# Matmul with batch norm on one core: two blocks of the third tile stored by GpSimd's converting transfers, one more raw block of the fifth tile, and a held half-block stored in two partition ranges

## The chip, the cores and the metric

The kernel runs on one core of one Trainium2 chip. The metric is the device time of one execution in microseconds (us). Three runs of the kernel before gave 205.51, 205.90 and 206.09 us, median 205.90. One further execution was profiled; its own numbers stand in the section on the profile below.

## The reference

The reference multiplies x (16 x 512 rows of 1024, float32) by a weight of 1024 x 768 and normalises each of the 768 output columns over all 8192 rows:

```python
y = np.matmul(x, weight)
mean = np.mean(y, axis=(0, 1), keepdims=True)
var = np.var(y, axis=(0, 1), keepdims=True)
y_norm = (y - mean) / np.sqrt(var + eps)
return (gamma * y_norm + beta).astype(np.float32)
```

No output of a column can be written before the whole column has been multiplied, since mean and variance need all its rows. The output is 25.17 MB of float32.

## The kernel before

The 768 columns are six tiles of 128, numbered 0 to 5; the 8192 rows are 16 chunks of 512. What the texts call the third tile is number 2, the fifth is number 4. GpSimd loads x with converting transfers (float32 in HBM, bf16 in SBUF, L404), VectorE transposes it (L429, L436), and TensorE multiplies. Tiles 0 and 1 are made together with rows on the partitions (L511); tiles 2 to 5 are made transposed, with the 128 columns on the partitions and 512 rows along the free dimension (L576). The multiplying goes on tile after tile, and while tile n is multiplied, tile n-1 is normalised and stored. Two chunks make a block of 1024 rows by 128 columns, 512 KB in float32; a tile has eight blocks, numbered by their first chunk 0, 2, 4 ... 14.

The work of one multiplied chunk: VectorE takes the statistics of the PSUM bank (L712), then ScalarE copies the bank to SBUF as bf16 (L716). There are eight PSUM banks. When the last chunk of a tile is in, its scale and shift are made (L977 to L1007), and then each block of it goes out in one of these ways, since the transposed result has to be turned back:

- **"xact"** (tiles 2 and 3): normalise in place (ScalarE L1024 for tile 2, VectorE L1027 for tile 3), a transposing DMA from SyncE into a bf16 slot of the SBUF ring (L1221), ScalarE converts that to a float32 slot of the ring (L1233), SyncE stores (L1203).
- **"xpool"** (no block of the kernel before): the same as far as the transposing DMA; then GpSimd stores the bf16 slot with a transfer that converts to float32 on its way (L1227). There is no float32 slot and no work for ScalarE.
- **"pe"** (tile 4): normalise in place (L1027), eight 128 x 128 transposes on TensorE (L1045), ScalarE copies the PSUM bank to a float32 slot (L1211), SyncE stores (L1203).
- **raw** (blocks listed in RAW): the bf16 block is turned by a transposing DMA before it is normalised (L1107); when scale and shift are known, they are spread over the partitions as rows (VectorE L1142 and L1143, seven small copies per tile on GpSimd or ScalarE L1146, ScalarE L1159), VectorE multiplies (L1175), GpSimd adds (L1179), SyncE stores (L1183).

The blocks of tiles 0 and 1 go out through VectorE and GpSimd (L938, L943) and SyncE (L947).

The last block of tile 4 is **held** (function held_block): its two halves of 512 rows are transposed on TensorE after the last matmul, copied by ScalarE (L1253) and stored by SyncE (L1256, 256 KB each) while the statistics of tile 5, the last, are finished (L1311 to L1327). Then tile 5 is normalised (L1351), transposed (L1045), copied (L1364) and stored in eleven pieces (L1367).

Work is put in order by a planner in the kernel (function arrange): each task has engines with a cost, a due time and the slots that it takes, and the planner deals the tasks out to the engines by its own costs. Each engine then runs its list in that order and waits on semaphores; a task that may run on one of two engines (L1146 and L548 among them) is put where the planner finds room. All stores of SyncE are in one list, and a transposing DMA in that list stands in line with the stores. The ring holds six float32 slots of a block; a slot comes free when the store that reads it has landed.

Of the kernel before, what the change touches and what calls it, by code (L numbers as in the profile page):

```python
# [227 lines left out]
def kernel(  # L228
# [9 lines left out]
    nc = tc.nc  # L238
# [9 lines left out]
    P = 128  # L248
# [19 lines left out]
    PAD = 50  # L268
    HELD = 1
    PAIRED = 1  # L270
    ASTAT = {2:tuple(range(4,16))}
    RC = C - 2
    XT, YB, SQ = C - EARLY, 29, 3
    ADDED = (0,6,16,28,40)
    PARTED, LATE, SINGLE = (4,5,7,8,9,10), (12,13,14,15), (2,3,6)
    MODE = {2:'xact',3:'xact',4:('pe',)*8}
    MODE = {nt: m if isinstance(m, tuple) else (m,) * (C // GY) for nt, m in MODE.items()}
    RAW, RAWADD, RAWDUE = {2:(0,2),3:(0,2),4:(0,2,4)}, {2:'POOL',3:'POOL',4:'POOL'}, {2:14.0,3:8.0,4:8.0}
    LAST = (12,13,14,15)
    SOON = ((11, {"POOL": (1.06, 1.1)}),)  # L280
    RING = 3 * CH // 32 * KQ // 2
# [3 lines left out]
    out_flat = out.flatten_outer_dims()  # L285
# [9 lines left out]
    def seq(bi):  # L295

        ins = bi.ins
        prev = last.get(ins.engine)
        if prev is not None:
            tc.add_manual_dep(  # L300
                ins, prev,
                mybir.DependencyInfo(mybir.DependencyClass.NoSync, mybir.DependencyReason.DATA),
                reason="order",
            )
        last[ins.engine] = ins.name
        return bi
# [21 lines left out]
    fin = singles.tile([P, 9 + 6 * len(PIECES)], f32)  # L328
    psums = {nt: singles.tile([P, 2, C], f32, name=f"psums{nt}") for nt in ASTAT}
    sums = {nt: singles.tile([P, 4 + 6 * C], f32, name=f"sums{nt}") for nt in ASTAT}  # L330
    for nt in ASTAT:
        seq(nc.vector.memset(sums[nt][:, 1:2], float(len(ASTAT[nt]) * CH)))
    msq = singles.tile([P, GA], f32)
# [23 lines left out]
    def task(prio, engines, emit, deps=(), lock=False, **kw):  # L357
        t = Task(prio, engines, emit, deps, **kw)
        t.lock = lock
        tasks.append(t)  # L360
        return t

    def dve(occ):
        return {"DVE": (occ, occ + 0.09)}

    def act(occ):
        return {"ACT": (occ, occ + 0.11)}
# [4 lines left out]
    def pe(occ):  # L372
        return {"PE": (occ, occ + 0.03)}
# [4 lines left out]
    def piece(slot):  # L378
        return ring[:, slot.at:slot.at + slot.words]
# [28 lines left out]
    def load_affine(eng):  # L408
        seq(nc.vector.memset(gamma_sb, 0.0))
        seq(nc.vector.memset(beta_sb, 0.0))  # L410
        for nt in range(0, NT, 2):
            n = 2 if nt < 2 * PAIRED else 1
            for i in range(nt, nt + 2, n):
# [35 lines left out]
    for kind, n, *n1 in order:  # L449
# [10 lines left out]
        rows = n1[0] if kind == "p" else QR if kind == "x" else CH  # L460
        m0 = n if kind == "p" else n * rows
        if m0 == M // 2:
            affine_loads = affine = task(t, {"SP": (5.0, 7.0)}, load_affine, [x_ready[m0 // CH - 3, 0, JW]])
        slot = Slot(rings, rows // 32 * KQ // 2)
# [221 lines left out]
    def y_of(nt, c):  # L686
        return y_col.setdefault((nt, c // GY), Slot(ys))
# [11 lines left out]
    def stats_of(nt):  # L699
        return stats[:, (nt - GA) * C:(nt - GA + 1) * C]  # L700
# [3 lines left out]
    def col_stats(nt, c, slot, t):  # L704
        now = clock[0]

        def bn(eng):
            dst = fin[:, 3:9] if (nt, c) == (NT - 1, C - 2) else stats_of(nt)[:, c, :]
            if nt in ASTAT:
                i = 4 + 6 * [j for j in range(C) if j not in ASTAT[nt]].index(c)  # L710
                dst = sums[nt][:, i:i + 6]
# [195 lines left out]
    def spread_rows(i):  # L907
        def emit(eng):
            a_ps = psum.tile([P, CH], f32, tag="b")
            aff[i] = a_ps[:, 0:NA]  # L910
            for a in range(GA):
                spread(a_ps[:, a * P:(a + 1) * P], (scale, shift)[i], a)
        return emit
# [11 lines left out]
    p0 = task(U, pe(0.45), spread_rows(0), [sc], takes=[a0_slot])  # L925
    p1 = task(U, pe(0.45), spread_rows(1), [sr], takes=[a1_slot])
# [93 lines left out]
    def norm(nt, c, n=1):  # L1020
        def emit(eng):
            part = y(nt, c, n)
            if eng == "ACT":
                seq(nc.scalar.activation(  # L1024
                    part, part, AF.Identity, bias=shift[:, nt:nt + 1], scale=scale[:, nt:nt + 1]))
            else:
                seq(nc.vector.tensor_scalar(  # L1027
                    part, part, scale[:, nt:nt + 1], shift[:, nt:nt + 1],
                    op0=ALU.mult, op1=ALU.add))
        return emit  # L1030

    def turn_block(prio, nt, m0, count, deps, uses):

        bank = Slot(banks)
        todo = []

        def step():
            if not todo:
                o_ps = psum.tile([P, count, P], bf16, tag="b")
                bank.tile = o_ps  # L1040
                for s in range(count):
                    c, i = divmod(m0 // P + s, RT)
                    todo.append((o_ps[:, s], y(nt, c)[:, i * P:(i + 1) * P]))
            dst, src = todo.pop(0)
            seq(nc.tensor.transpose(dst, src, ident))  # L1045

        def emit(eng):
            for _ in range(emit.task.count):
                step()

        emit.step = step
        t = task(prio, pe(0.0555 * count), emit, deps, takes=[bank], uses=uses)
        emit.task = t
        turns[t] = [count, count]
        return t, bank
# [136 lines left out]
    def col_block(nt, c, due, fin_task, held=False):  # L1192
# [12 lines left out]
        a = task(due, act(1.144) if nt == GA else dve(0.45), norm(nt, c, GY), [fin_task] + keeps, nt > GA, uses=[yslot])  # L1205
        if MODE[nt][c // GY] == "pe":
            b, bank = turn_block(due + 0.5, nt, m0, count, [a], [yslot])
# [11 lines left out]
        def xbar(eng):  # L1219
# [3 lines left out]
        b = task(due + 0.5, {"SP": (1.4, 1.4)}, xbar, [a], dma=XBAR,  # L1223
                 takes=[t_slot] + ([slot] if MODE[nt][c // GY] == "xact" else []), uses=[yslot])
        if MODE[nt][c // GY] == "xpool":
            def store_x(eng):
                seq(nc.gpsimd.dma_start(dst(), t_slot.o))  # L1227
# [13 lines left out]
    def held_block(nt, c, due, fin_task, last_mm, root_task):  # L1241
        yslot = y_of(nt, c)
        keeps = [col_end[nt, c + i][1] for i in range(GY)]
        count = RT
        a = task(due - 20.0, dve(0.45), norm(nt, c, GY), [fin_task] + keeps, True, uses=[yslot])
        for i in range(GY):
            slot = Slot(rings, count * P)
            m0 = (c + i) * CH
            b, bank = turn_block(due - 1.0 + 0.1 * i, nt, m0, count, [a, last_mm], [yslot])

            def copy(eng, slot=slot, bank=bank):
                slot.o = piece(slot).rearrange("p (s n) -> p s n", n=P)
                seq(nc.scalar.copy(slot.o, bank.tile))  # L1253

            def store(eng, slot=slot, m0=m0):
                seq(nc.sync.dma_start(  # L1256
                    out_flat[m0:m0 + count * P, nt * P:(nt + 1) * P].rearrange("(s p) n -> p s n", p=P), slot.o))

            d = task(due - 60.0 + 15.0 * i, act(0.48), copy, [b] + ([root_task] if i else []), takes=[slot], uses=[bank])
            task(due, {"SP": (0.38, 0.4)}, store, [d], dma=count * P * P * 4 / 1024 * STORE * 1.024, uses=[slot])  # L1260
# [35 lines left out]
    nt = NT - 1  # L1296
# [45 lines left out]
    for c, r0, rows in ends:  # L1342
        due = E + 2.0 + 0.6 * c
        n = max(rows // CH, 1)
# [11 lines left out]
        m0 = c * CH + r0  # L1356
        count = rows // P
        b, bank = turn_block(due + 0.6 * (n - 1), nt, m0, count, norms, [y_of(nt, c + i) for i in range(n)])
        slot = Slot(xts)
# [55 lines left out]
```

## Time and profile before

| what | value |
|---|---|
| median of three runs | 205.90 us (205.51 to 206.09) |
| the profiled execution, its own time | 206.26 us |
| its span, first to last instruction | 204.5 us |
| mean granted TensorE clock | 0.974 |
| PE busy / DVE / ACT / POOL | 190.6 / 159.1 / 145.4 / 129.9 us |
| HBM read / written | 36.71 MB / 25.17 MB |
| transposing DMAs | 12 at L1221, 7 at L1107 |
| stores of 512 KB from the ring, of 256 KB | 37, 6 |
| converting copies on ScalarE (L1233) | 12 |

PE is TensorE, DVE VectorE, ACT ScalarE, POOL GpSimd and SP SyncE, which only issues DMAs. Times in the profile count from the start of the span. "GB/s" is what the core's 16 DMA engines moved, "DMA share" their mean busy share; since an engine can have two packets open, the share goes over 1. A group row reads: line, engine, operation, out<-in, shapes, count, then busy us, mean ns of one, and idle time before it with what ended it. The chain of work that ended last reads: start, duration, what. The trace also holds every DMA packet with its start, duration and size; each store ends with one packet of 4 bytes from every DMA engine that took part, called an end mark here.

### The profile page before, as it was taken

The page shows a single profiled execution, that of the slowest core. Times are in us where ns is not written, and L with a number is a line of the kernel's source. Part 1 is how long each engine was busy: PE and PEld are TensorE (multiplying, and loading weights), DVE is VectorE, ACT ScalarE, POOL GpSimd, SP SyncE. Part 2 cuts the span into 40 slices and gives each one's busy share as a digit, 9 for nine tenths or more (in the row PEclk, how much of TensorE's full clock was granted, in tenths as well). Part 3 has the DMA queues.
Part 4 walks back from the last instruction along what each step waited for, and adds up shares of the span by engine and source line. Part 5 has one row for each costly group of instructions (what it writes and reads, how often), then busy time and mean ns, then how long its engine had stood idle before and what let it go on. Part 6 is the DMA issues. An engine that isn't in the chain of part 4 may idle for free.

```text
span 204.5 us, 3512 instructions
## 1 busy us (share of the span) xinstructions
PE 190.6 (93%) x1210; PEld 116.5 (57%) x1210; DVE 159.1 (78%) x249; ACT 145.4 (71%) x260; POOL 129.9 (64%) x155
## 2 busy tenths in 40 slices
PE   7989999999999999999999999999999999997900
PEld 3467554747488888777866444444444445544900
DVE  4031879999999998969979998987997998657800
ACT  2000460369979999899976866999998769946940
POOL 7776954877499989996933999389612902940000
PEclk9999999999999999999999999999999999999685
DMA  5999999999999999999689999999999999999997
GB/s 75 140 201 197 189 196 196 196 198 196 190 194 197 197 196 197 196 197 195 105 182 192 347 338 337 258 295 326 294 313 178 291 332 295 347 343 330 313 346 230
DMA packets 98562, 48.74 MB, mean 238 GB/s; under 512 B 24304, under 2 KB 98032, under 8 KB 98544
## 3 DMA queue, kind: packets, MB, share of 16 engines
q0 software_dynamic: 34624, 18.36, 65.3%
q1 hardware_dynamic: 63920, 30.16, 54.5%
q8 instruction: 9, 0.15, 0.3%
q14 instruction: 9, 0.07, 0.1%
HBM read 36.71 MB, written 25.17 MB: 303 GB/s over the span
## 4 chain that ended last, share of the span: by engine, by line
PE 83%; DMA 6%; ACT 3%; POOL 2%; issue 1%; ACTq 0%; DVE 0%; POOLq 0%
PE y_ps L576 52%; PE y_ps L511 23%; DMA w_sb<-in_weight_dram 6%; PE y_ps L815 4%; ACT o_sb L1364 3%; PE o_ps L1045 1%; POOL ring L404 1%; PE y_ps L754 1%; POOL w_sb L388 1%; PE a_ps L904 1%; PE o_ps L1075 0%; ACTq L1410 0%; PE tot_ps L872 0%; ACT ring L1253 0%; DVE y_sb L1351 0%
## 5 line engine op out<-in xcount | busy, mean ns | idle before, releaser
L576 PEld LDWEIGHTS <-w_sb 128*128 128x128 bf16 x520 | 50.4, 97 | 57.2
L576 PE MATMUL y_ps<-x_pl,w_sb 128*128 128x512 bf16 x280 | 63.8, 379 | 0.0
L404 POOL DMA_DIRECT2D ring<-in_x_dram x76 | 47.2, 626 | 14.3 <-DMA ring<-in_x_dram 5.4
L511 PE MATMUL y_ps<-w_sb,xT_sb 128*128 128x256 bf16 x448 | 50.7, 273 | 1.1 <-DMA ring<-in_x_dram 0.9
L576 PE MATMUL y_ps<-xT_sb,w_sb 128*128 128x512 bf16 (+1 forms) x240 | 51.6, 369 | 0.0
L511 PEld LDWEIGHTS <-xT_sb 128*128 128x128 bf16 x448 | 43.5, 98 | 8.9 <-DVE xT_sb L436 2.1
L436 DVE STREAM_TRANSPOSE xT_sb<-ring 128x1024 f32<-128x1024 f32 (+1 forms) x29 | 31.2, 1111 | 14.2 <-DMA ring<-in_x_dram 14.0
L712 DVE BATCH_NORM_STATS2 stats<-y_ps 128x6 f32<-128x512 f32 x46 | 30.8, 686 | 6.4 <-PE y_ps L576 6.3
L548 ACT COPY x_pl<-xT_sb 128x1024 bf16<-128x1024 bf16 x33 | 33.6, 1064 | 1.7 <-DVE xT_sb L436 1.7
L716 ACT CAST y_sb<-y_ps 128x512 bf16<-128x512 f32 x51 | 28.6, 593 | 8.5 <-DVE stats L712 4.9
L943 POOL TENSOR_TENSOR ring<-ring,sum 128x1024 f32<-128x1024 f32 (+1 forms) x11 | 23.7, 2190 | 11.0 <-DVE ring L938 10.9
L660 ACT ACTIVATE sq_sb<-y_ps 128x512 f32<-128x512 f32 x28 | 16.4, 614 | 17.3 <-PE y_ps L511 16.7
L667 POOL TENSOR_TENSOR sum<-sum,sq_sb 128x512 f32<-128x512 f32 x20 | 25.5, 1276 | 3.5 <-ACT sq_sb L660 2.4
L663 DVE TENSOR_TENSOR sum<-y_ps,sum 128x512 f32<-128x512 f32 x28 | 18.9, 675 | 6.5 <-ACT sq_sb L660 5.5
L673 ACT CAST y_sb<-y_ps 128x512 bf16<-128x512 f32 x28 | 16.1, 601 | 8.0 <-DVE sum L663 7.8
L1179 POOL TENSOR_TENSOR ring<-ring,sum 128x1024 f32<-128x1024 f32 x7 | 17.1, 2460 | 7.2 <-DVE ring L1175 5.2
L938 DVE TENSOR_TENSOR ring<-y_sb,a_ps 128x1024 f32<-128x1024 bf16 (+1 forms) x16 | 16.7, 1080 | 0.1
L1045 PE MATMUL o_ps<-ident,y_sb 128*128 128x128 bf16 x104 | 13.7, 249 | 1.6 <-DVE y_sb L1351 1.5
L1146 POOL COPY sum<-sum 32x256 f32<-32x256 f32 (+1 forms) x17 | 5.5, 325 | 13.8 <-ACT sum L1146 7.0
L1233 ACT CAST ring<-ring 128x1024 f32<-128x1024 bf16 x12 | 12.6, 1054 | 1.6 <-DMA ring<-y_sb 1.6
L429 DVE STREAM_TRANSPOSE xT_sb<-ring 128x2048 bf16<-128x2048 bf16 x6 | 13.5, 2289 | 0.2 <-DMA ring<-in_x_dram 0.2
L592 PE MATMUL idle_ps<-idle_sb 128*128 128x512 f32 x18 | 10.5, 741 | 1.5 <-DVE idle_sb L318 1.5
(105 smaller groups left out, 159.6 us busy)
## 6 DMA issues: line engine op xcount, KB each, us to landing
out_dram<-ring SPq DMA_DIRECT2D x37, 512.0 KB, 3.6
ring<-in_x_dram POOLq DMA_DIRECT2D x52, 256.0 KB, 8.8
out_dram<-o_sb SPq DMA_DIRECT2D x6, 512.0 KB, 5.1
ring<-in_x_dram POOLq DMA_DIRECT2D x16, 128.0 KB, 6.0
w_sb<-in_weight_dram POOLq DMA_DIRECT2D x8, 192.0 KB, 6.2
out_dram<-ring SPq DMA_DIRECT2D x6, 256.0 KB, 3.1
ring<-in_x_dram POOLq DMA_DIRECT2D x4, 192.0 KB, 8.1
out_dram<-o_sb SPq DMA_DIRECT2D x3, 256.0 KB, 2.9
```

The lines of the kernel that those rows point to most:

```text
L404: bi = seq(nc.gpsimd.dma_start(x_bf[32 * i:32 * i + 32], src[:, :, KQ * i:KQ * (i + 1)]))
L436: seq(nc.vector.transpose(dst, src[:, :, jw0:jw1]))
L511: seq(nc.tensor.matmul(y_ps[:, s], x_of(c, jw, e, t * P, (t + 1) * P), w_sb[:, jw, e, 0:NA], start=(s == 0 and jw == 0 and e == 0), stop=( ...
L548: seq(nc.scalar.copy(dst, pairs) if eng == "ACT" else ENG[eng].tensor_copy(dst, pairs))
L576: seq(nc.tensor.matmul(y_ps, w_sb[:, jw, e, nt * P:(nt + 1) * P], moving(c, jw, e, q0 * QR, q1 * QR, parted), start=(jw == 0 and e == 0 an ...
L663: seq(nc.vector.tensor_add(sum1, slot.tile[:, 0:n], sum1))
L667: seq(ENG[eng].tensor_add(acc, acc, state["sq"][:, 0:n]))
L712: seq(nc.vector.bn_stats(dst, slot.tile))
L716: seq(nc.scalar.copy(y(nt, c), slot.tile))
L938: seq(nc.vector.tensor_mul(slot.o, y_row[c].y[:, s0:s1], aff[0][:, None, :].to_broadcast([P, n, NA])))
L943: seq(ENG[eng].tensor_add(slot.o, slot.o, row[:, None, :].to_broadcast([P, n, NA])))
L1179: seq(ENG[eng].tensor_add(slot.o, slot.o, row[:, None, :].to_broadcast([P, n, P])))
```

## The change

Three settings and one function change. MODE gives blocks 4 and 8 of tile 2 (places 2 and 4 of the tuple) to "xpool" instead of "xact". RAW gets block 6 of tile 4, which was a "pe" block. In held_block, the store of the second half is split by partitions: 108 of them in one DMA, the other 20 in another. Since the planner deals with all tasks together, other instructions move as well.

```diff
     PAIRED = 1
+    CUT = 108
@@
-    MODE = {2:'xact',3:'xact',4:('pe',)*8}
+    MODE = {2:('xact','xact','xpool','xact','xpool','xact','xact','xact'),3:'xact',4:('pe',)*8}
@@
-    RAW, RAWADD, RAWDUE = {2:(0,2),3:(0,2),4:(0,2,4)}, {2:'POOL',3:'POOL',4:'POOL'}, {2:14.0,3:8.0,4:8.0}
+    RAW, RAWADD, RAWDUE = {2:(0,2),3:(0,2),4:(0,2,4,6)}, {2:'POOL',3:'POOL',4:'POOL'}, {2:14.0,3:8.0,4:8.0}
@@
-            def store(eng, slot=slot, m0=m0):
-                seq(nc.sync.dma_start(
-                    out_flat[m0:m0 + count * P, nt * P:(nt + 1) * P].rearrange("(s p) n -> p s n", p=P), slot.o))
+            def store(eng, slot=slot, m0=m0, cuts=(0, P) if i == 0 else (0, CUT, P)):
+                rows = out_flat[m0:m0 + count * P, nt * P:(nt + 1) * P].rearrange("(s p) n -> p s n", p=P)
+                for p0, p1 in zip(cuts, cuts[1:]):
+                    seq(nc.sync.dma_start(rows[p0:p1], slot.o[p0:p1]))
```

In the changed program's lists, TensorE has 96 transposes at L1045 instead of 104. ScalarE loses two copies of L1233, one of L1211 and one of L548, and gets 13 of the small copies of L1146. VectorE loses one L1027 and gets one L1175 and one L548. GpSimd loses those 13 small copies and gets one L1179 and two storing DMAs. SyncE loses three stores of L1203 and gets one transposing DMA of L1107, one store of L1183 and one held store. (From L271 on, line numbers of the changed kernel are one higher, after held_block's store two.)

## The prediction

> **What bounds the kernel now.** I read the chain that ended last first. TensorE carries it without a break from 110.77 until the last tile is multiplied, and the list of TensorE's waits between 111 and 186 us is empty.
>
> ```profile
> 110.77 58.70 PE y_ps L576 x269
> ...
> 177.67 0.21 PE y_ps L576
> 177.89 0.06 PE o_ps L1045
> 177.94 6.91 PE y_ps L576 x32
> 184.85 1.81 PE y_ps L754 x16
> 186.66 0.24 PE o_ps L1045 x4
> ...
> 188.64 0.54 PE o_ps L1045 x4
> 189.18 0.04 issue
> 189.22 0.41 PE o_ps L1045 x4
> 189.63 0.02 issue
> 189.65 5.66 ACT o_sb L1364 x7
> ```
>
> To see: matmuls alternate with transposes of tile 4's "pe" blocks, 0.06 us each, up to 177.94; then two units, the last statistics, and ScalarE's copies. The chain ends at 196.71, though, nearly 8 us before the span of 204.5. What runs there is in the table by stretches (PE, PEld, DVE, ACT, POOL busy; clock; DMA share; GB/s):
>
> ```profile
> 155.00:157.00 2.00, 2.00 (x11) 0.88 (x9) 1.20 (x3) 2.00 (x5) 0.00 (x0) 1.00 1.29 138
> 157.00:159.50 2.50, 2.50 (x13) 1.18 (x12) 2.38 (x3) 1.38 (x2) 1.02 (x1) 1.00 1.58 115
> ...
> 174.00:188.00 14.00, 13.11 (x86) 7.24 (x84) 8.85 (x18) 9.64 (x16) 6.89 (x3) 1.00 1.15 346
> ...
> 188.00:188.50 0.50, 0.00 (x0) 0.00 (x0) 0.46 (x3) 0.49 (x2) 0.00 (x0) 1.00 0.73 206
> ...
> 190.00:191.50 1.50, 1.50 (x18) 1.29 (x17) 1.50 (x6) 1.50 (x3) 0.00 (x0) 0.70 0.78 233
> 191.50:196.00 4.50, 3.27 (x37) 3.09 (x34) 2.18 (x7) 4.50 (x6) 0.00 (x0) 0.72 1.15 346
> 196.00:202.00 6.00, 0.00 (x0) 0.00 (x0) 0.00 (x0) 0.72 (x2) 0.00 (x0) 0.62 1.15 347
> ```
>
> To see: 346 GB/s is what the DMAs give with these stores; they give it from 174 to 188 and again from 191.5 to the end. In between they fall to 206 and 233. So most DMA engines wait for the first store of tile 5, and then tile 5's 4.19 MB take 12.1 us: here the end hangs on the chain.
>
> For one DMA engine that isn't so. End marks of the last 512 KB store before the held block lie at 188.17 to 188.40 for 14 engines, at 189.00 for one and at 189.58 for one. That last one's next marks are 190.34, 191.09, 191.48, 191.86, 192.62: steps of 0.755 for 256 KB and 0.378 for 128 KB, exactly its pace under load. It never idles, and at the end its mark is at 203.21 where 15 others lie at 202.68 to 202.83. I call it **the late engine**; the program's end is its end. It fell behind when it fetched instructions: one packet of 16,384 bytes on queue q8 at 180.11 took 0.95 us, after which one engine's mark is missing from its batch.
>
> SyncE's list shows the load on the queue before:
>
> ```profile
> 180.39 2.05 SPq L1183 DMA_DIRECT2D out_dram<-ring  x1
> ...
> 183.97 1.40 SPq L1183 DMA_DIRECT2D out_dram<-ring  x1
> 187.58 1.04 SPq L1256 DMA_DIRECT2D out_dram<-ring  x2
> 189.36 10.51 SPq L1367 DMA_DIRECT2D out_dram<-o_sb  x11
> ```
>
> To see: issuing a store takes 1.4 us and more where 0.37 is usual, so the queue is full; the last store of tile 4 before the held block goes in at 183.97.
>
> **Part 1, the raw block, on TensorE.** It removes eight transposes. From 169.47 to 177.94 the chain holds 31 transposes and 31 matmuls in 8.47 us, 0.273 a pair; a matmul alone is 6.91 / 32 = 0.216. So a transpose costs 0.057, eight 0.46 us, on the chain, with no wait behind which it could hide. Everything after, to the first store of tile 5, comes 0.46 us sooner if TensorE still never waits.
>
> Other engines, from these rows:
>
> ```profile
> L1233 ACT CAST ring<-ring 128x1024 f32<-128x1024 bf16 x12 | 12.6, 1054 | 1.6 <-DMA ring<-y_sb 1.6
> L1179 POOL TENSOR_TENSOR ring<-ring,sum 128x1024 f32<-128x1024 f32 x7 | 17.1, 2460 | 7.2 <-DVE ring L1175 5.2
> L1146 POOL COPY sum<-sum 32x256 f32<-32x256 f32 (+1 forms) x17 | 5.5, 325 | 13.8 <-ACT sum L1146 7.0
> ```
>
> ScalarE loses 2 x 1.054 (L1233), 1.015 (L1211) and 1.064 (L548), 4.2 us; it gains four small gathers at 0.243 and nine spreading copies, which its own trace does not show: between 0.243 (its gather) and 0.411 (GpSimd's row), so 3.2 to 4.7. Even. VectorE: +1.216 (L1175), +0.716 (L548), -0.541 (L1027), +1.4 us. In the trace it took the statistics of a unit ready at about 155.5 only at 159.39, and TensorE never waited; the eight banks are the cover, and I count nothing. If the cover is gone, each us of lateness beyond it is a us of TensorE.
>
> **Part 2, the DMA queue.** The added L1107 transfer is 256 KB in packets of 256 bytes. Landings of such transfers queued back to back lie 0.97 apart (170.35, 171.32): +1.0 us of every DMA engine. It stands in SyncE's list behind three L1221, near the start of tile 3's blocks; the stores behind it wait for it.
>
> The two converting stores move 512 KB each. The trace has converting transfers inward only. Bounds: as much as an ordinary 512 KB store, 1.51 us, or as the loads per 512-byte packet written (196 GB/s instead of 347), 2.7 us: 0 to +2.3 us together. I take 0, nearer to a store's own write side. They cost GpSimd two issues, 0.63 (L404, half the rows) to 1.25 each, behind waits for the L1221 landings; queued behind them are the last two L943 and then the L1179, and SyncE's L947 and L1183 wait for those. GpSimd stood idle 3.5 us at 128 and 5.7 at 146, and gives up 13 small copies, about 4.6 us net of four that stay. These stores would leave at about 134 and 139, where tile 2's same blocks now leave at 135.07 and 143.36, in a stretch where the queue has gaps (233 GB/s from 128 to 132). Against that, in the changed list tile 2's raw products (L1175) stand behind the twelfth statistics of tile 3, about 148, not at 139.68 and 142.41: two stores some 6 to 9 us later.
>
> By 160 the list would have put out eight stores of tile 2, against seven now, with one transfer more: about half a store ahead against 1.0 us. The stretch from 155 to 159.5 loses some 2.9 us to transposing transfers that stall; whether that comes back, no row says. So the late engine's queue up to the held block ends later by m, with m from -0.3 to +3.3 (1.0 + 2.3). It can't end much sooner: the last L1175 now stands behind the third last statistics (181.0 + 0.6), ends at 182.8, its L1179 (2.36) at 185.2, and an issue there lands 2.8 to 3.6 later, at 188 to 189. I take m = +0.2.
>
> **Part 3, the split.** On each engine an even half-block costs 0.755 (32 packets of 23.6 ns). The trace has no uneven store. Bounds for the late engine: spared its whole share, -0.755; given twice its share, +0.755. Every store here deals equal shares; 108 deals equally to 12 engines at most (9 partitions, 36 packets), 20 to 10 (8 packets). So some engines get 44 packets, +0.28, and four none, -0.755. Is the late engine among those four? In the order of the marks within a batch its mark was about the 13th of 16, so I take -0.755. The extra issue (0.37) lies in SyncE's idle time before 189.36.
>
> The Trainium skill ("DMA: Bandwidth & Descriptors", section on why a DMA increments its semaphore by 16) says a SyncE transfer takes the largest number up to 16 that divides its slowest dimension, and the lowest-numbered engines; that would give 12 and 10 and spare the last four. No run shows it yet. Its rules for kernel authors speak against such a split: two transfers to disjoint partitions only serialize. By that rule the split would give 0 instead of -0.755.
>
> **The sum.** Late engine: 203.21 + 0.2 - 0.755 = 202.66, -0.55. The 15 others: the chain lets them start 0.46 sooner, 202.83 - 0.46 = 202.37; those with 44 packets are ready for tile 5 at 188.3 + 0.2 + 0.755 + 1.04 = 190.3, just when it now comes (190.78 - 0.46). So -0.55 for the span, 206.26 - 0.55 = 205.7 for the profiled execution, which was 0.36 above the median of the runs: **205.35 us** for the median.
>
> **Rivals.**
> - *A, the late engine is not spared.* Then its end moves by +0.28 + m = +0.5, whatever TensorE gains: 206.4. For: the 13th place is in time, not a number of the engine. Against: four of 16 have nothing to do, and the place fits them. Were the late engine one of two with 36 packets, +0.1 + m: 206.2.
> - *B, the queue grows (slower).* Place: SyncE's stores between 150 and 188, full already. Price: 1.0 for the transposing transfer, plus up to 2.3 for conversion, plus the late raw stores. From m = 0.75 on nothing is left of the split's gain; with m = 2.0 the late engine ends 1.25 later, 207.1. Against: the gaps before 136, one store fewer to do at 160.
> - *C, the stall at 155 to 159.5 is smaller.* Then m = -0.3, and the others' chain is the limit: -0.8, 205.1.
> - *D, the relief doesn't reach TensorE.* ScalarE's small copies stand before the copies of banks near 154 to 158; if TensorE waits 1 us, the chain is +0.5, the others end at 203.4: 206.1 to 206.6.
>
> **Chances and numbers.** 0.3% (0.62 us) is about what a measurement of this kernel can tell from no change. Forecast 0.45 (faster by more 0.27, within 0.18); A 0.17 (within 0.09, slower 0.08); B 0.20 (slower 0.18, within 0.02); C 0.12 (faster 0.10, within 0.02); D 0.06 (slower 0.04, within 0.02). Together faster 0.37, within 0.33, slower 0.30. The range goes from C less 0.3 for the runs' own spread, 204.8, to B, 207.1.
>
> **What would show it.** Right: 96 transposes, the last unit of TensorE ending near 186.2 instead of 186.66 with no waits; the two converting stores in GpSimd's list before 142; in the tail, four engines without end marks for the 108 and 20 partitions, and all 16 last marks within 0.3 us. Wrong: a mark at the end later than its batch by 0.5 or more (A); the last L1183 store landing after 190.5 (B); idle time on TensorE before 186 (D).

## The result, and the profile after

The changed kernel takes 208.34 us (median of six runs, 208.09 to 208.55) where the kernel before takes 205.70: ratio 1.0129 [1.0112, 1.0147]. It is 2.6 us slower, outside the predicted range of 204.8 to 207.1. The profiled execution of the changed kernel took 208.09 us, with a span of 206.3 and a granted clock of 0.979. In the changed kernel a line of the code is numbered one to three higher (product L1176, addition L1180, SyncE's stores L1204 and L1184, converting copy L1234, spread L1147, converting store L1228).

First the chain that ended last, as before. The profile now follows it back to 171.28 us only; these are five of its pieces (start, duration, what):

```profile
171.30 0.40 ACT sum L1147
...
172.96 0.19 ACT ring L1234
...
177.81 5.01 DMA out_dram<-ring
...
184.51 1.22 DVE ring L1176
...
189.77 0.36 DVE y_sb L1353
```

To see: from 171.28 on it no longer runs along TensorE until the last tile's transposes. It goes through ScalarE's dealing of the fifth tile's factors (L1147), the converting copies behind it, a store that holds a ring slot for 5.01 us, and the last raw product of VectorE at 184.51, behind which the last statistics stand; so the last tile is normalised from 189.77. TensorE itself waits once only, after its last unit. That is from the waits of TensorE between 100 and 200 us (the page of the profile has 96 transposes, as forecast):

```profile
PE o_ps L1046 <- DVE y_sb L1353: 3.8, 1, 3.8
```

Now the stretches (columns as in the prediction, GB/s last) and SyncE's list:

```profile
173.00:174.00 1.00, 1.00 (x9) 0.57 (x8) 0.00 (x0) 1.00 (x2) 0.00 (x0) 1.00 0.70 156
174.00:175.00 1.00, 1.00 (x9) 0.60 (x8) 0.96 (x1) 1.00 (x3) 0.00 (x0) 1.00 0.02 7
```

```profile
170.35 1.66 SPq L1222 DMA_TRANSPOSE ring<-y_sb  x1
174.03 4.15 SPq L1204 DMA_DIRECT2D out_dram<-ring  x4
```

To see: SyncE issues nothing from 172.0 (170.35 + 1.66) to 174.03, and the DMA engines, with all that was in their queue written, do 156 and then 7 GB/s. In the kernel before the same two microseconds have 332 and 346, because SyncE issues four stores from 171.91 on; ScalarE has made the first of these copies at 170.84. The two stretches, SyncE's list and ScalarE's list of the kernel before:

```profile
173.00:174.00 1.00, 1.00 (x10) 0.54 (x8) 1.00 (x2) 1.00 (x3) 0.18 (x1) 1.00 1.14 332
174.00:175.00 1.00, 1.00 (x9) 0.54 (x8) 0.29 (x1) 1.00 (x3) 1.00 (x1) 1.00 1.15 346
```

```profile
171.91 4.46 SPq L1203 DMA_DIRECT2D out_dram<-ring  x4
```

```profile
170.84 1.04 ACT L1233 CAST ring<-ring 128x1024 f32<-128x1024 bf16 x1
```

The hole of the changed kernel is (347 - 156) + (347 - 7) = 531 KB, 1.5 us at 347 GB/s. I counted the output that is still to be written from the store packets of the trace. 14 us before TensorE's last unit ends, every kernel of this study has 9.85 to 10.19 MB left, about 19 blocks: whatever happened earlier, they lie within 0.34 MB, 1.0 us at 347 GB/s. The changed kernel has 10.19, the kernel before 9.96. 6 us before that end, it is 8.25 MB in the changed kernel and 7.36 MB in the kernel before: 0.89 MB more, 2.6 us at 347 GB/s. From there both write at the same mean rate (327 and 329 GB/s up to the last store packet), so this is the loss: 0.23 MB of it is older than that first point, 172 us in the changed kernel, and 0.66 MB is lost in the eight us behind it.

The table uses a mark that all kernels share, the end of the matmuls of L815 (105.31 in the kernel before, 104.77 in the changed one); executions begin their matmuls up to 1.2 us apart, and this takes it out. "Factors" is the aggregate of the fifth tile's statistics on VectorE (L977), "left" the MB to write 6 us before the last unit's end. The last four columns come from one profiled execution each, and these scatter: e12 differs from e1 by one load at the start, and its factors and last packet lie 1.2 and 1.0 us later. Differences of about 1 us in these columns therefore prove little by themselves. The ratios are from all runs; losses in us that are given with a percentage are worked out from them.

| kernel | ratio to before | last unit ends | last store packet | factors | left |
|---|---|---|---|---|---|
| before | 1 | 81.36 | 97.87 | 59.5 | 7.36 |
| after | 1.0129 [1.0112, 1.0147] | 81.20 | 100.27 | 61.6 | 8.25 |
| e1 raw block alone | 1.0016 [1.0002, 1.0030] | 80.91 | 97.60 | 59.5 | 7.42 |
| e2 converting stores alone | 1.0092 [1.0076, 1.0108] | 81.58 | 99.69 | 61.7 | 7.79 |
| e3 split alone | 1.0034 [1.0020, 1.0049] | 81.36 | 98.02 | 59.5 | 7.30 |
| e4 raw block and split | 1.0018 [1.0002, 1.0034] | 80.91 | 97.73 | 59.5 | 7.61 |
| e5 split, semaphores as before | 1.0027 [1.0011, 1.0042] | 81.67 | 98.53 | 59.9 | 7.32 |
| e6 converting stores, early products | 1.0077 [1.0054, 1.0100] | 81.36 | 99.33 | 59.6 | 7.73 |
| e7 before with late products | 1.0050 [1.0032, 1.0068] | 81.36 | 98.83 | 60.9 | 7.65 |
| e8 after with early products | 1.0060 [1.0039, 1.0080] | 80.91 | 98.76 | 59.6 | 7.93 |
| e9 converting stores in the old places | 1.0200 [1.0177, 1.0222] | 84.14 | 101.02 | 63.0 | 7.47 |
| e10 after, two copies first | 1.0096 [1.0076, 1.0116] | 81.18 | 99.46 | 61.6 | 8.05 |
| e11 before, spread dealt as in after | 1.0073 [1.0052, 1.0095] | 81.40 | 99.50 | 60.3 | 7.90 |
| e12 raw block, semaphores as before | 1.0008 [0.9994, 1.0021] | 81.81 | 98.61 | 60.7 | 7.45 |
| e13 as e9, buffers that nobody awaits | 1.0049 [1.0032, 1.0067] | 82.11 | 99.03 | 61.0 | 7.50 |
| e14 after, spread as in before | 1.0101 [1.0079, 1.0122] | 81.20 | 99.94 | 61.6 | 7.76 |
| e15 after, one VectorE copy moved | 1.0109 [1.0091, 1.0126] | 80.91 | 99.58 | 61.0 | 8.15 |

### The profile page after: what moved, and what is told of

Its sections match the earlier page's. It is cut to its first block, busy times and chain, and to the rows that moved or that the text cites. A ratio compares the mean times of both kernels' runs of the same rounds, so it can differ in the third digit from the quotient of the medians.

```text
span 206.3 us, 3500 instructions
## 1 busy us (share of the span) xinstructions
PE 189.8 (92%) x1202; PEld 116.0 (56%) x1202; DVE 161.9 (78%) x250; ACT 146.2 (71%) x269; POOL 129.8 (63%) x145
## 5 line engine op out<-in xcount | busy, mean ns | idle before, releaser
L1180 POOL TENSOR_TENSOR ring<-ring,sum 128x1024 f32<-128x1024 f32 x8 | 18.8, 2358 | 25.9 <-DVE ring L1176 21.8
L549 ACT COPY x_pl<-xT_sb 128x1024 bf16<-128x1024 bf16 x32 | 32.8, 1060 | 1.7 <-DVE xT_sb L437 1.7
L713 DVE BATCH_NORM_STATS2 stats<-y_ps 128x6 f32<-128x512 f32 x46 | 30.1, 682 | 2.3 <-PE y_ps L577 2.3
L1046 PE MATMUL o_ps<-ident,y_sb 128*128 128x128 bf16 x96 | 11.5, 250 | 3.9 <-DVE y_sb L1353 3.8
L1176 DVE TENSOR_TENSOR ring<-r_sb,a_ps 128x1024 f32<-128x1024 bf16 x8 | 9.6, 1216 | 6.9 <-ACT ring L1234 1.8
L1234 ACT CAST ring<-ring 128x1024 f32<-128x1024 bf16 x10 | 10.3, 1053 | 0.7 <-DMA ring<-y_sb 0.7
```

The lines of the kernel that those rows point to most:

```text
L549: seq(nc.scalar.copy(dst, pairs) if eng == "ACT" else ENG[eng].tensor_copy(dst, pairs))
L713: seq(nc.vector.bn_stats(dst, slot.tile))
L1180: seq(ENG[eng].tensor_add(slot.o, slot.o, row[:, None, :].to_broadcast([P, n, P])))
```

## The experiments

**The three parts one by one.** Each kernel has one part of the diff, or two, and leaves the rest as before.

> Only the fifth tile's raw block is added; no converting store, no split. In the changed kernel VectorE's last raw product waited 1.66 us for a slot in front of the last statistics. Theory R (the raw block is the cause: one transfer more in the queue and one product more in front of the statistics): at least +1.0 us on the kernel before, with a wait of VectorE before its last product of 1 us or more. Theory X (the converting stores and the order they bring are the cause): -0.5 to +0.3 us, as my prediction's own sum for this part, with no such wait above 1 us.

> Only the two converting stores; no added raw block, no split. Theory X: +1.5 us or more on the kernel before; the queue runs dry around 146 to 150 and 172 to 176 us as in the changed kernel. Theory R: within 0.5 us of the kernel before, since two copies of ScalarE are saved and the bytes are the same.

> Only the split of the second held half into 108 and 20 partitions; no instruction order changes otherwise. If the late engine is among the four without a share: -0.2 to -0.4 us, and the last store's end marks lie within 0.3 us. If it is not: +0.2 to +0.4 us, with one mark 0.6 or more behind its batch. Neither theory R nor X expects more than that of it.

> The added raw block and the split, without the converting stores. Theory R: +0.8 us or more on the kernel before, near the raw block alone. Theory X: -0.8 to +0.2 us, that is the gain which I predicted for the whole change, since TensorE's eight transposes are gone and the late engine is relieved.

Measured: 206.16, 207.69, 206.53 and 206.12 us where before takes 205.78. So the converting stores carry 1.9 of the 2.6 us, as theory X has it; in e2 the queue falls to 138 GB/s from 146 to 148 us and to 255 from 172 to 176. e1 and e4 lie just above theory X's bands (+0.38 and +0.34 us), far under theory R's, and in e1 VectorE waits 0.7 us at most before a raw product after 160 us. The raw block does on TensorE what was forecast (80.91 instead of 81.36, 0.45 us), but the times show nothing of it. The split costs 0.75 us, more than either of its two cases said.

**The split, and how the program ends.** In e1 and e3 the span ends 1.35 us after the last landing, in the kernel before 0.92. At the end SyncE waits for its eight DMA semaphores, one after the other in a fixed order, 0.06 us each; they are dealt to its transfers in turn. With 88 transfers the last store has the last one waited for, with 89 the first, and then seven waits still follow its landing (7 x 0.06 = 0.42). Two other kernels fit: with 86 transfers (e2, two waits follow) it is 1.05 us, with 90 (e4, six follow) 1.30. The changed kernel has 88, and 0.93 us. Setting PAIRED to 2 loads gamma in one transfer less:

```diff
-    PAIRED = 1
+    PAIRED = 2
```

> The split alone again, but two of gamma's loads are made one, so that SyncE issues as many DMAs as the kernel before. The split alone cost +0.75 us. In its profile the last store landed on the first of the eight semaphores that SyncE waits for at the end, and seven more waits of 0.06 us followed, +0.43 us from landing to end against the kernel before. Theory L (the count of DMAs decides how many waits follow the last landing): 0.3 to 0.5 us less than the split alone, so +0.2 to +0.4 us on the kernel before, the rest being the late engine's larger share. Rival (the split costs by its stores alone): unchanged, +0.6 to +0.9 us.

> The raw block alone (206.16 us, landing to end of the span 1.35 us), and one pair of transfers regrouped at the start so that the number of SyncE's transfers, and with it the semaphore of the last store, is that of the kernel before. Theory (SyncE ends by waiting for eight semaphores in a fixed order, and the wait for the last store's came first of them): 0.3 to 0.5 us less than the raw block alone, 205.6 to 205.9 us, landing to end 0.92 us. Rival (the order of the waits costs nothing): 206.0 to 206.4 us.

Measured: landing to end falls from 1.35 to 0.92 in both. The times are 206.32 (ratio 1.0027 against 1.0034 without it) and 205.84 (1.0008 against 1.0016). The traces show the 0.43 us; by the ratios the times move by 0.15 in that direction, with overlapping intervals, so for the time it isn't settled: e5, 0.62 us over the kernel before, lies in the rival's band, e12 in the theory's.

**The order of the third tile's raw products.** In the changed kernel they stand at 146.92 and 148.04 us on VectorE, before at 139.68 and 142.41. RAWDUE sets when the planner wants them (14.0 in both kernels of the diff).

```diff
-    RAW, RAWADD, RAWDUE = ..., {2:14.0,3:8.0,4:8.0}
+    RAW, RAWADD, RAWDUE = ..., {2:10.0,3:8.0,4:8.0}
```

(The dots stand for the settings of RAW and RAWADD, which stay. 10.0 is in e6, made from e2, and in e8, made from the changed kernel; e7 is the kernel before with 22.0.)

> The two converting stores alone, with the due time of the third tile's raw products 4 us earlier (10 for 14), which puts their L1175 behind the sixth and ninth statistics of the fourth tile, near their place before (seventh and ninth), not behind the twelfth. The converting stores alone cost +1.9 us. Theory O (the order that they bring is the cause: late raw products, a queue that runs dry near 146 us, more stores left for the end): within 0.7 us of the kernel before. Theory C (the converting transfers are the cause, by holding up the queue around 137 to 142): still +1.4 us or more.

> The kernel before with the due time of the third tile's raw products 8 us later (22 for 14), which puts their L1175 behind the twelfth and fourteenth statistics; no converting store, no added raw block, no split. Theory O: +1 us or more on the kernel before, with the queue dry near 146 us. Theory C: within 0.5 us of the kernel before.

> The whole change with the third tile's raw products due 4 us earlier, which puts them behind the sixth and ninth statistics. Theory O: 1.5 us or more below the changed kernel, 205.8 to 206.8. Theory C: within 0.7 us of the changed kernel, 207.6 or more.

Measured: 207.34, 206.98 and 206.97 us. e7 has no converting store and loses 1.0 us (0.50%) by order alone, as theory O has it; its second product stands at 152.20, though, 4 us later than in the changed kernel. In its profiled execution the factors come 1.3 us later, and the stretch from 172 to 176 us shows the gap.

```profile
172.00:176.00 4.00, 3.95 (x32) 2.23 (x31) 1.52 (x2) 3.96 (x7) 0.60 (x2) 1.00 0.87 251
```

e8 gets 1.4 us (0.69%) back with the factors where they were, between the two theories and near O. In e6 the factors are back as well, but only 0.3 us is, with overlapping intervals, and its time is in theory C's band. There SyncE's stores come 2.4 to 2.5 us apart (170.79, 173.19, 175.69), and ScalarE's copies end 2.2 to 2.4 us apart where the kernel before has 1.3 to 1.4. So late factors don't explain the loss alone.

**The converting stores in the old places.** In e9 and e13 every instruction keeps its place in the lists of the kernel before; the two ScalarE copies are left out and the two stores go from SyncE's list to GpSimd's.

```diff
+            def store_x(eng):
+                seq(nc.gpsimd.dma_start(dst(), t_slot.o))
...
+            if nt == 2 and c in (4, 8):
+                placed.extend([(d, lambda eng: None), (e, store_x)])
...
+    for t, emit in placed:
+        t.emit = emit
```

> The kernel before, with every instruction in the place it has there, but blocks 2 and 4 of the third tile are stored by GpSimd's converting transfers: their two ScalarE copies (L1233) are gone and their two stores stand in GpSimd's list at the places the plan gave SyncE's. Theory R (the converting stores cost nothing much by themselves; the time is lost because the planner, given the freed ScalarE time and GpSimd's added time, re-deals the later work): within 0.3% of the kernel before, 205.4 to 206.3 us, and the stretch 172 to 176 us keeps over 300 GB/s. Theory X (the transfers themselves cost it, by conversion or by GpSimd's waits): like the two stores alone, 207.3 to 207.9 us.

Measured: 209.82 us, 4.1 us (2.0%) over the kernel before: twice what the part costs alone, and beyond both theories. SyncE's waits (128 to 176 us) and TensorE's say why:

```profile
SPq L1221 <- DMA out_dram<-ring: 8.0, 2, 4.1
```

```profile
PE o_ps L1045 <- DVE y_sb L1027: 2.6, 1, 2.6
```

To see: a transposing transfer writes where the bf16 block lies that the converting store still reads. The copy that it replaces frees that slot in 1.05 us; the store holds it until it lands, 4.4 and 5.6 us. Twice SyncE waits some 4 us for it, and in the end TensorE stalls for 2.6. e13 gives the two bf16 blocks the buffer that the float32 block would have had:

```diff
+            held_by = slot if nt == 2 and c in (4, 8) else t_slot
+            t_slot.o = piece(held_by)[:, 0:count * P // 2].bitcast(bf16)...
```

> The kernel before with blocks 2 and 4 of the third tile stored by GpSimd's converting transfers in the places of the old stores, as in the run before, but their transposed halves lie in the buffer that the converted block would have had, so no later transfer waits for them. Theory H (what cost 4.1 us there was the hold on the buffers: SyncE waited 8.0 us for their landing): 205.3 to 206.3 us, within 0.3% of the kernel before, and no wait of SyncE's transposing transfers for a store. Theory X (the transfers themselves cost it, by their packets or by GpSimd's list): 207.3 us or more.

Measured: 206.85 us. SyncE's wait is gone, and with it 3 of the 4 us; 1.0 us (0.49%) remains, between the two theories. What is left: two transposing transfers issued beside the first converting store land 5.9 and 6.0 us after their issue (before 3.9 and 4.2), the second keeps SyncE 3.39 us in its issue (before 1.80), and VectorE's list is 1.5 us late at the factors. TensorE waits for VectorE there once, as below. (The profiled execution, 207.65 us, is the slowest of the nine, so it may show more than the usual loss.)

```profile
PE o_ps L1045 <- DVE y_sb L1027: 0.6, 1, 0.6
```

**The dealing of the spread.** In the changed kernel the planner put the fifth tile's gather on GpSimd and its dealing out on ScalarE, in front of two converting copies; before it was the other way. e11 forces that on the kernel before, e10 takes only the two copies ahead of the dealing in the changed kernel, e14 gives the spread back to the engines that had it.

```diff
-        s = task(now, {"POOL": (1.2, 1.25), "ACT": (1.0, 1.1)}, deal, [g])
+        s = task(now, {"ACT": (1.0, 1.1)} if nt == 4 else {"POOL": (1.2, 1.25), "ACT": (1.0, 1.1)}, deal, [g])
...
+    order[at:at] = ahead
+    late.engine, named("gather")[-1].engine = "POOL", "ACT"
```

(The first two lines are e11's, with the gather bound to GpSimd in the same way; the third is in e10 and e14, the fourth in e14 alone.)

> The kernel before with one assignment forced: the fifth tile's factors are gathered by GpSimd and dealt out by ScalarE, in front of its two last converting copies, as the planner did it in the changed kernel. Theory R: these copies come 1 to 2 us later, the queue has less to write at 172 to 176 us, and the time is 206.6 to 207.4 us. Rival (the order of these copies is a mark of the loss, not its cause): 205.5 to 206.1 us.

> The changed kernel with one thing moved: ScalarE's last two converting copies of the fourth tile stand in front of its three spreading copies and the bank copy for the fifth tile's factors, no longer behind them. Theory R, and these two copies as the place (SyncE has no store to issue from 169.7 to 174.0 us and the queue runs dry): 1 to 2 us under the changed kernel, 206.3 to 207.3 us, with over 280 GB/s from 172 to 176 us. Rival (the spread is then 2 us late, so the fifth tile's products are, and the gap only moves on to 176 to 180 us): 208.0 to 208.6 us.

> The changed kernel with the fifth tile's spread dealt as in the kernel before: ScalarE gathers (four copies of 0.24 us), GpSimd deals out, and ScalarE's two converting copies stand in front of the bank copy. Theory R, if the new dealing is the larger part of the loss: 206.2 to 207.0 us and over 300 GB/s from 172 to 180 us. Rival (the dealing costs only what the two copies gave back; the rest is stores that are late for another reason): 207.4 to 208.0 us.

Measured, in the order of the texts: e11 207.31, e10 207.69 and e14 207.87 us. One line for e11, one for e10 and two for e14:

```profile
172.00:176.00 4.00, 4.00 (x32) 2.29 (x30) 1.93 (x3) 3.98 (x7) 0.00 (x0) 1.00 0.55 159
```

```profile
176.00:180.00 4.00, 4.00 (x26) 2.00 (x24) 3.19 (x5) 3.63 (x6) 3.61 (x2) 1.00 0.91 271
```

```profile
172.00:176.00 4.00, 3.95 (x30) 2.30 (x30) 2.66 (x4) 3.53 (x6) 1.52 (x3) 1.00 1.18 333
...
186.00:188.00 2.00, 0.56 (x10) 0.39 (x7) 1.47 (x6) 1.62 (x5) 0.83 (x1) 1.00 0.91 267
```

To see: put into the kernel before, this one dealing makes the hole and costs 1.5 us (0.73%). In e10, with the copies ahead of it, and in e14, with the dealing taken back, the hole closes (333 for 208 GB/s from 172 to 176 in both), but the queue then runs dry elsewhere: from 176 to 180 in e10, from 186 to 188 in e14, where also one DMA engine ends 0.76 us behind the others. They win back 0.7 and 0.6 us by their ratios, about what the runs can tell. So the dealing is enough to make a loss, and undoing it isn't enough to mend it: my theory that the dealing is the larger part fell.

**A VectorE copy that takes five times its time.** In all kernels in which the planner placed the converting stores, one copy of x stands beside GpSimd's second issue (VectorE, then GpSimd, changed kernel):

```profile
136.56 3.79 DVE L549 COPY x_pl<-xT_sb 128x1024 bf16<-128x1024 bf16 x1
```

```profile
136.49 0.91 POOL L1228 DMA_DIRECT2D out_dram<-ring  x1
137.42 2.38 POOL L944 TENSOR_TENSOR ring<-ring,sum 128x1024 f32<-128x1024 f32 x1
```

It takes 0.69 elsewhere; here it ends 0.55 us after GpSimd's addition. The Trainium skill (SBUF — State Buffer, section on who interferes with whom) says that such a copy and a GpSimd instruction exclude each other for the whole instruction; the trace agrees (3.79 us for 0.69), and here the copy ends only behind two GpSimd instructions in a row, the issue of a transfer and the addition. e15 moves the copy behind the next statistics.

> The changed kernel with one VectorE copy (L549) moved behind the next statistics, so that it no longer starts beside GpSimd's issue of the second converting store, where it took 3.79 us instead of 0.69. Theory S (this stall is the root of the late stores): at least 1 us under the changed kernel, 207.3 us or less, and the fifth tile's factors (VectorE L978) come 2 us sooner against TensorE's end. Theory O (the lists' order decides; VectorE has made the 3.1 us up when it waits for TensorE at 151.5 us): 208.0 to 208.6 us, the factors at the same place, 19.6 us before TensorE's last unit ends. By the Trainium skill (SBUF - State Buffer, section on who interferes with whom) a VectorE copy of this kind and a GpSimd instruction exclude each other; where the copy now starts beside GpSimd's addition alone, it would wait for that one's end, at most 1.5 us.

Measured: 207.65 us, where before took 205.52; 2.1 us over it instead of 2.6, between the two theories, with intervals that overlap. The copy now takes 2.06, ending 0.56 after the addition:

```profile
138.37 2.06 DVE L549 COPY x_pl<-xT_sb 128x1024 bf16<-128x1024 bf16 x1
```

The hole stays (202 GB/s from 172 to 176) and the factors come 0.6 us sooner, not 2. So this stall is at most a small part: at 151.5 us VectorE waits for TensorE in both kernels (1.03 us), and its next statistics start at the same place, 46.72 us behind the end of L815.

## Why the prediction was wrong

- **Part 1, TensorE: right.** "eight 0.46 us, on the chain": 0.45 in e1, e4 and e8. In the changed kernel 0.3 of it is lost again, some of it in idle time around 170 us (3.88 of 4.00 busy from 168 to 172). The times of e1, e4 and e12 show no gain, so their end doesn't hang on it alone. "Everything after, to the first store of tile 5, comes 0.46 us sooner" didn't come in the changed kernel: the last tile is normalised from 189.77 instead of 188.24, with the 0.54 between the ends of L815 2.1 us later.
- **Part 2, the queue: the step that failed,** "I take m = +0.2". The last L1184 store lands at 191.90, the last L1183 before at 189.98; with the 0.54 between the ends of L815, m is +2.5. It was inside the bounds (-0.3 to +3.3), and rival B, with m = 2.0, is the case that came: its mark, "the last L1183 store landing after 190.5", is there. B's 207.1, the top of the range, still had the split's -0.755 in it; 205.9 + 2.5 without it gives 208.4, and 208.34 was measured. In the prediction's own steps it is the last raw product that fails: it was to end at 182.8 and its store to land "at 188 to 189". It ended at 185.73, since VectorE waited in front of it for ScalarE's list, and that list for a ring slot (the store of 5.01 us in the chain above):

```profile
184.51 1.22 DVE L1176 TENSOR_TENSOR ring<-r_sb,a_ps 128x1024 f32<-128x1024 bf16 x1 [1.66 <-ACT y_sb L717]
```

  Three things of the sum were wrong.
  - I added up transfers from 128 us on. The 1.0 us for the transposing transfer is not in the time of e12 (ratio 1.0008, 0.2 us), where the waits at the end are as before: what the queue carries before 172 us is nearly made up there, where all kernels have about 19 blocks left.
  - Most of the loss comes after that point (0.66 of 0.89 MB): when the fifth tile's factors are ready and in which order the engines then supply blocks. This is VectorE's row of before, then after:

```profile
164.84 0.59 DVE L977 BATCH_NORM_AGGREGATE mv<-stats 128x2 f32<-128x96 f32 x1
```

```profile
166.40 0.59 DVE L978 BATCH_NORM_AGGREGATE mv<-stats 128x2 f32<-128x96 f32 x1
```

  With the 0.54 between the ends of L815 it is 2.1 us later. I saw the planner's new order (the raw products "behind the twelfth statistics"), counted it as two late stores, and for VectorE's added work wrote "I count nothing", because TensorE had cover. TensorE had; SyncE had not. e7 shows that such an order alone costs 0.50%, 1.0 us, e11 the same for the spread (0.73%, 1.5 us). That it acts through the factors is read from the traces and not shown: e6 has them in time and still loses 1.6 us.
  - "I take 0" for the conversion: in the old places, with buffers that nobody awaits, the two stores cost 1.0 us (e13), in the lower half of the bounds 0 to 2.3. A converting store of the changed kernel lands 5.5 us after its issue (median) against 3.5 for SyncE's 512 KB stores from the ring, and its slot is held as long.

```profile
out_dram<-ring POOLq DMA_DIRECT2D x2, 512.0 KB, 5.5
```

- **Part 3, the split: rival A's case.** "so I take -0.755": the number of engines was right, the place wrong. End marks of SyncE's queue count 3,504 before and 3,510 in e3, that is 12 + 10 for one store of 16. That agrees with the Trainium skill's rule that I cited (DMA: Bandwidth & Descriptors, why a DMA increments its semaphore by 16) as far as the counts go; which engines they are, no trace shows. But in e3 two engines end 0.35 and 0.58 us behind the middle of their batch, where the late one of the kernel before ends 0.48 behind. In the changed kernel one engine ends at 205.06, the 15 others at 204.52 to 204.76, so the 0.3 us that I gave as the sign of being right was not met there either. That the late one got the larger share fits the last mark in e3: followed back by its own steps, its share of the split store ends at 190.77, 1.08 us after 189.69, and 44 packets take 1.04. The place among the marks of a batch is no number of the engine. The split alone is 0.3% slower. The Trainium skill's rules for kernel authors, on the same page, speak of two partition halves that each use all 16 engines; by them I had put the split's worth at 0, and its cost here is more than that.
- **B's place was too wide,** "SyncE's stores between 150 and 188": three quarters of the loss are made between 172 and 180. C's stall was in fact smaller (from 155 to 157 and 157 to 159.5 us 343 and 159 GB/s instead of 138 and 115), but the end is no sooner for it. D didn't come: TensorE has no wait before its last unit.

What stays open: how the 2.6 us divide. The parts alone add up (0.92 + 0.34 + 0.16 = 1.42% against 1.29%), but within the converting stores I can name a cost of their own (e13: 1.0 us), the order of the raw products (e7: 1.0) and the dealing (e11: 1.5), each enough by itself for a loss of that size in the kernel before, and no run in which undoing them gives all of it back; the most is 1.4 us (e8). Each new order has its own empty stretch; why e6 loses 1.6 us with its factors in time was only read from its list, not tried.

## What to carry to other kernels

Find the last point at which the queue has caught up with what is ready; in this kernel a cost of 1.0 us ahead of it did not show in the time. Behind it look for the first block that comes late and for what its engine does before it. Where a planner deals out the work, a removed task is a new order for all engines: compare the lists from that point on before any transfer is priced. A transfer that replaces a copy holds its source until it lands, so ask who needs that buffer next.

## What the runs showed that I had not expected

- The order in which SyncE waits for its semaphores at the end makes up to 0.43 us in the traces: 1.35 against 0.92 from the last landing to the end of the span.
- GpSimd's issue of a transfer followed by an addition held a VectorE copy of 0.69 us for 3.79.
